# Stick-breaking attention: transposes two pieces behind the scores, contractions in quarters, and the causal mask on GpSimd

## The chip, the cores and the metric

The kernel runs on one core of a Trainium2 chip. Its engines are TensorE (PE for matmuls, PEld for its weight loads), VectorE (DVE), ScalarE (ACT), GpSimd (POOL) and SyncE (SP, which issues the DMAs). The metric is the device time of one execution in microseconds.

## What is computed

One decoder layer in float32 over 1024 tokens of width 1024: three token mixers beside each other (stick-breaking attention, mLSTM, cross-attention into a memory), merged by gates, and then a gated MLP. The change lies in the stick-breaking attention of 8 heads of width 64:

```python
z = einsum('bhtd,bhsd->bhts', q_block, k[:t1]) * scale
strict = arange(t1)[None, :] < (t0 + q_pos)[:, None]
log_fail = where(strict, log_sigmoid(-z), 0.0)
log_after = cumsum(log_fail, axis=3, reverse=True) - log_fail
w = where(strict, exp(log_sigmoid(z) + log_after), 0.0)
out = einsum('bhts,bhsd->bhtd', w, v[:t1])
```

A query sees earlier keys alone, strictly. For a masked key the factor sigmoid(-z) has to be 1 and the weight 0.

## The kernel before

The sequence is held in reverse, so the running product over later keys becomes a scan from left to right. Heads are worked in pairs (`p` = 0 to 3). A pair's scores are cut into 12 pieces, `PIECES`: a block of 128 queries (`rb`) by up to 512 keys (`o` is the first key block, counted from the diagonal; `w` is the width in keys). With `o == 0` a piece holds the diagonal block in its first 128 columns; that is so in 8 of 12 pieces, 32 of 48 in all.

One piece passes through these steps:

- `sb_weights`: scores of both heads on TensorE into the PSUM tile `z` (one buffer of two banks), each as two matmuls with split operands (L410, L413). On the diagonal a matmul of the identity with `mask` (0 or -1e30) stands between them (L412). ScalarE makes `f` = sigmoid(-z/8) (L415) and `g` = sigmoid(z/8) (L416), each in a buffer of the ring `U` (5 buffers). The first column of `f` is 1, by a memset on GpSimd (L418), or the carry of the piece before (L420). VectorE scans `f` to running products, one scan per head (L422), and multiplies `g` by them (L424).
- `sb_turn`: TensorE transposes `g` by blocks of 128 into the PSUM tile `tr` (one buffer, L434), ScalarE copies it to `y` (L436).
- `sb_apply`: TensorE contracts `y` with V (`sbv`) into the bank `pv` (L448); a finished bank is copied by ScalarE and stored (`store_y`, L395, L396).

Between these steps TensorE gets other work by generators, `chunks`: the projections of the next pair's Q and K (`proj_chunks`; evicted by `eq` and `ek` on ScalarE and VectorE), in the last pair the mLSTM's V (`nat_chunks`). A projection of one 512-wide half is 24 matmuls of three products (`mm3`, L149 to L151). A generator pauses after `k == 3` and at its end, so a chunk is half a contraction, 12 matmuls.

The loop over pieces (L604 to L625) sets the order in which instructions are written: scores, then a chunk in two of three pieces, then `apply_two` when two pieces are transposed, then the transposes of the piece before. A scheduler places the instructions engine by engine, near that order; weight loads have higher priority. Each engine works its queue in order. Behind the attention `gx_part` prepares the operands of the gate products, with four chunks drawn after each part.

Of the kernel before, what the change touches and what calls it, by code (L numbers as in the profile page):

```python
# [11 lines left out]
F32R = mybir.dt.float32r  # L12
AF = mybir.ActivationFunctionType
ALU = mybir.AluOpType
# [4 lines left out]
P = 128  # L19
# [10 lines left out]
NCH = S // P  # L30
# [12 lines left out]
def tile_hybrid_layer(ctx: ExitStack, tc: tile.TileContext, xT, memT, vecs, w_t, w_n, w_kv, w_if,  # L43
# [4 lines left out]
    nc = tc.nc  # L48
# [56 lines left out]
    def ts(t):  # L105
# [5 lines left out]
    ident_r = const.tile([P, P], F32R, tag="ident", name="ident")  # L111
    nc.vector.tensor_copy(ident_r, raw_id)
    ident = ident_r.bitcast(F32)

    raw_mask = T([P, P], "hf")
    nc.gpsimd.memset(raw_mask, 0.0)
    nc.gpsimd.affine_select(out=raw_mask, in_=raw_mask, pattern=[[1, P]], compare_op=ALU.is_gt, fill=-1e30,
                            base=0, channel_multiplier=-1)
    mask_r = const.tile([P, P], F32R, tag="mask", name="mask")
    nc.vector.tensor_copy(mask_r, raw_mask)  # L120
    ones = const.tile([P, P], F32, tag="ones", name="ones")
    nc.vector.memset(ones, 1.0)
    ones_r = const.tile([P, 2], F32R, tag="ones_r", name="ones_r")
# [211 lines left out]
    def proj_chunks(src, consume, halves=(1, 0)):  # L335

        with tc.high_priority(offset=SOON):
            wh, wl = wsplit(src)
        for h in halves:
            p = bank("pj")  # L340
            for k in range(KT):
                mm3(p, wh[:, ts(k)], wl[:, ts(k)], hh[k][:, hs(h)], hl[k][:, hs(h)], k == 0, k == KT - 1)
                if k == 3:
                    yield
            consume(h, p)
            yield

    def nat_chunks(which, consume, order=range(NCH - 1, -1, -1), ws=()):
        with tc.high_priority(offset=SOON):
            ws = list(ws) + [wsplit(w_n[which, b], None if b < 2 or ws else "pg") for b in range(len(ws), 4)]  # L350
        for t in order:
            p = bank("pj")
            for k in range(KT):
                wh, wl = ws[k // 2]
                mm3(p, hh[k][:, ts(t)], hl[k][:, ts(t)], wh[:, hs(k % 2)], wl[:, hs(k % 2)],
                    k == 0, k == KT - 1)
                if k == 3:
                    yield
            consume(t, p)
            yield  # L360
# [43 lines left out]
    def sb_weights(p, st, rb, o):  # L404
        qs, ks, kz = st
        w = min(4, NCH - rb - o) * P
        c = slice((rb + o) * P, (rb + o) * P + w)
        z = two("z")
        for a in range(2):
            nc.tensor.matmul(z[:, a, :w], qs[a][:, ts(rb)], ks[a][:, c], start=True, stop=False)  # L410
            if o == 0:
                nc.tensor.matmul(z[:, a, :P], ident_r, mask_r, start=False, stop=False, skip_group_check=True)  # L412
            nc.tensor.matmul(z[:, a, :w], qs[a][:, ts(rb)], kz[a][:, c], start=False, stop=True)  # L413
        f, g = T([P, 2, HALF + 1], "U"), T([P, 2, HALF], "U")
        nc.scalar.activation(f[:, :, 1:w + 1], z[:, :, :w], AF.Sigmoid, scale=-0.125)  # L415
        nc.scalar.activation(g[:, :, :w], z[:, :, :w], AF.Sigmoid, scale=0.125)  # L416
        if o == 0:
            nc.gpsimd.memset(f[:, :, 0:1], 1.0)  # L418
        else:
            nc.vector.tensor_copy(f[:, :, 0:1], carry[0])  # L420
        for a in range(2):
            nc.vector.tensor_tensor_scan(f[:, a, 1:w + 1], f[:, a, 1:w + 1], f[:, a, 1:w + 1],  # L422
                                         1.0 if o == 0 else f[:, a, 0:1], op0=ALU.mult, op1=ALU.bypass)
        nc.vector.tensor_mul(g[:, :, :w], g[:, :, :w], f[:, :, 0:w])  # L424
        carry[0] = f[:, :, w:w + 1]
        return g
# [45 lines left out]
    st, chunks = sb_qk(0)  # L472
# [116 lines left out]
        nc.sync.dma_start(v_d[t], v)  # L589


    weights, turned = [], []

    def turn_next():
        if weights:
            p, rb, o, g = weights.pop(0)
            turned.append((p, rb, o, sb_turn(rb, o, g)))

    def apply_two():
        if len(turned) == 2:  # L600
            for _ in range(2):
                sb_apply(*turned.pop(0))

    for p in range(4):  # L604
        now = st
        if p < 3:
            st, chunks = sb_qk(p + 1)
            chunks = chunks()
        else:
            chunks = nat_chunks(1, ev_v, [0, 1, 2, 3, 7, 6, 5, 4])  # L610
        for n, (rb, o) in enumerate(PIECES):
            g = sb_weights(p, now, rb, o)
            if n % 3 < 2:
                next(chunks, None)
            if (p, n) == (0, 2):
                next(rows_step)
            apply_two()
            turn_next()
            weights.append((p, rb, o, g))
        if p < 3:  # L620
            for _ in chunks:
                pass
    apply_two()
    turn_next()
    apply_two()  # L625

    spare.clear()
# [301 lines left out]

    for j in range(2):  # L930
        gx_part(j)
        for _ in range(4):
            next(chunks)
    go(3)
    LONG[:], SHORT[:] = ["pj"], ["pv"]
# [476 lines left out]
```

## Time and profile before

| what | value |
|---|---|
| runs, median (lowest to highest) | 1672.52 us (1671.65 to 1674.3) |
| profiled execution: time / span | 1671.65 us / 1669.6 us |
| TensorE matmuls busy | 1644.9 us (99%) |
| VectorE busy | 1209.9 us (72%) |
| ScalarE busy | 826.2 us (49%) |
| GpSimd busy | 53.4 us (3%) |
| scores of the attention, first to last start | 114.4 to 321.1 us |

Busy is the time in which at least one instruction of the engine runs. A matmul's duration covers its way through the array, while the next starts earlier: of matmuls in a row the distance of their starts is what each takes of TensorE's time. In rows of a timeline the columns are start, duration, engine, line, operation, output and inputs, shape, count, and in brackets the engine's idle time before it and what ended that.

### The profile page before, as it was taken

Reading aid. Unit: us, or ns where it says so; the run is one execution under the profiler, and the core shown is the slowest. Engines: PE = TensorE matmul, PEld = TensorE weight load, DVE = VectorE, ACT = ScalarE, POOL = GpSimd, SP = SyncE. Lnnn points to the kernel's source line nnn. Section 1 sums busy time; section 2 is a strip of 40 time slices with the busy share of each in tenths; the row PEclk is TensorE's granted clock in tenths of the full one; section 3 lists DMA queues with packets and bytes.
Section 4 is the critical chain, followed back from the end, with each engine's and each line's share of the span. In section 5 each row is a group of like instructions: output and inputs, shape, how many; then the busy total and the mean of one; then the engine's idle time right before and its main releaser. Section 6 shows DMA issues by size and latency. Waiting matters only on the chain.

```text
span 1669.6 us, 21196 instructions
## 1 busy us (share of the span) xinstructions
PE 1644.9 (99%) x7975; PEld 1338.8 (80%) x7975; DVE 1209.9 (72%) x1710; ACT 826.2 (49%) x1249; POOL 53.4 (3%) x95
## 2 busy tenths in 40 slices
PE   8999999999999999999999999999999999999999
PEld 4777777788877888888788888688888888788887
DVE  5648778777765666666567658997778877789864
ACT  4547667645555445656412334555555544543431
POOL 1000000010000001100000000000000000000000
PEclk9999999999999999999999999999999999999999
DMA  8421011234324665433855354222222221487141
GB/s 297 148 65 28 31 39 51 95 116 138 108 106 156 183 183 168 145 120 108 280 185 171 127 183 139 95 100 97 75 77 76 89 88 51 167 324 240 34 143 69
DMA packets 96249, 212.69 MB, mean 127 GB/s; under 512 B 12416, under 2 KB 36224, under 8 KB 96148
## 3 DMA queue, kind: packets, MB, share of 16 engines
q1 hardware_dynamic: 96148, 211.35, 37.3%
q8 instruction: 63, 1.03, 0.3%
q14 instruction: 38, 0.31, 0.1%
HBM read 156.71 MB, written 54.61 MB: 127 GB/s over the span
## 4 chain that ended last, share of the span: by engine, by line
PE 89%; DVE 4%; ACT 3%; DMA 2%; issue 1%; SPq 0%; POOLq 0%; ACTq 0%; DVEq 0%
PE ps_pj L149 14%; PE ps_pj L150 14%; PE ps_pj L151 14%; PE ps_pv L150 6%; PE ps_pv L151 6%; PE ps_pv L149 6%; PE ps_tr L149 4%; PE ps_tr L151 4%; PE ps_tr L150 4%; PE ps_z L149 3%; PE ps_z L150 3%; PE ps_z L151 3%; PE ps_tr L434 2%; PE ps_pv L448 1%; PE ps_z L226 1%; PE ps_z L413 1%
## 5 line engine op out<-in xcount | busy, mean ns | idle before, releaser
L150 PE MATMUL ps_pj<-h,whi 128*128 128x512 f32 x620 | 242.3, 391 | 0.0
L136 ACT ACTIVATE whi<-raw 128x512 fp32r<-128x512 f32 (+1 forms) x112 | 93.7, 836 | 180.3 <-PE ps_pj L150 84.8
L149 PE MATMUL ps_pj<-h,whi 128*128 128x512 f32 x412 | 163.0, 396 | 0.7 <-DVE U L1054 0.7
L149 PE MATMUL ps_pj<-pg,whi 128*128 128x512 f32 x396 | 154.7, 391 | 0.2 <-DVE pg L1052 0.2
L151 PE MATMUL ps_pj<-pg,wlo 128*128 128x512 f32 x380 | 148.0, 390 | 0.0
L150 PEld LDWEIGHTS ps_pj<-h,whi 128*128 128x128 f32 x620 | 116.5, 188 | 23.6 <-DVE U L287 0.2
L151 PE MATMUL ps_pj<-h,wlo 128*128 128x512 f32 x332 | 129.7, 391 | 0.0
L811 DVE SCALAR_TENSOR_TENSOR y<-U,vec,y 128x1023 f32<-128x1023 f32 x88 | 112.5, 1280 | 8.4 <-ACT y L809 8.4
L422 DVE TENSOR_TENSOR_SCAN U<-U 128x512 f32<-128x512 f32 (+3 forms) x96 | 88.6, 965 | 30.7 <-ACT U L415 29.8
L149 PEld LDWEIGHTS ps_pj<-h,whi 128*128 128x128 f32 x412 | 77.4, 188 | 17.2 <-DVE U L1054 1.1
L137 DVE TENSOR_TENSOR wlo<-raw,whi 128x1024 fp32r<-128x1024 f32 x54 | 66.0, 1223 | 30.8 <-ACT whi L136 30.6
L149 PEld LDWEIGHTS ps_pj<-pg,whi 128*128 128x128 f32 x396 | 74.4, 188 | 16.1 <-issue 0.5
L151 PEld LDWEIGHTS ps_pj<-pg,wlo 128*128 128x128 f32 x380 | 71.4, 188 | 14.9 <-issue 0.2
L136 ACT ACTIVATE whi<-pg 128x512 fp32r<-128x512 f32 (+1 forms) x59 | 43.4, 738 | 74.0 <-issue 21.2
L150 PE MATMUL ps_pj<-pg,whi 128*128 128x512 f32 x188 | 73.4, 390 | 0.0
L151 PEld LDWEIGHTS ps_pj<-h,wlo 128*128 128x128 f32 x332 | 62.4, 188 | 12.9
L150 PE MATMUL ps_pv<-h,whi 128*128 128x512 f32 x164 | 64.0, 390 | 0.0
L809 ACT ACTIVATE y<-U,vec 128x1024 f32<-128x1024 f32 x44 | 54.6, 1241 | 15.9 <-DVE U L713 14.4
L151 PE MATMUL ps_pj<-h,whi 128*128 128x512 f32 x156 | 60.8, 390 | 0.0
L137 DVE TENSOR_TENSOR wlo<-raw,wlo 128x512 fp32r<-128x512 f32 x58 | 39.9, 688 | 23.0 <-ACT wlo L136 22.9
L151 PE MATMUL ps_tr<-pg,wlo 128*128 128x512 f32 x144 | 56.2, 390 | 0.3 <-DVE wlo L137 0.3
L137 DVE TENSOR_TENSOR whi<-raw,whi 128x512 fp32r<-128x512 f32 x58 | 39.9, 688 | 21.8 <-ACT whi L136 21.8
(438 smaller groups left out, 4308.4 us busy)
## 6 DMA issues: line engine op xcount, KB each, us to landing
raw<-in_w_t_dram SPq DMA_DIRECT2D x29, 512.0 KB
gate_d<-U SPq DMA_DIRECT2D x24, 512.0 KB
U<-gate_d SPq DMA_DIRECT2D x24, 512.0 KB
pg<-in_w_up_dram SPq DMA_DIRECT2D x22, 512.0 KB
act_d<-y SPq DMA_DIRECT2D x22, 512.0 KB
pg<-in_w_t_dram SPq DMA_DIRECT2D x21, 512.0 KB
raw<-in_w_dn_dram SPq DMA_DIRECT2D x18, 512.0 KB
raw<-in_w_o_dram SPq DMA_DIRECT2D x16, 512.0 KB
```

Source lines behind the costliest of these rows:

```text
L136: nc.scalar.activation(hi, src, AF.Copy)
L137: (eng or nc.vector).tensor_sub(lo, src, hi.bitcast(F32))
L149: nc.tensor.matmul(out, lh, rh, start=start, stop=False, skip_group_check=more)
L150: nc.tensor.matmul(out, lh, rl, start=False, stop=False, skip_group_check=more)
L151: nc.tensor.matmul(out, ll, rh, start=False, stop=stop, skip_group_check=more)
L226: nc.tensor.matmul(pm[m], mg[k // 4][:, c], w[:, hs(kk)], start=(k == 0), stop=(k == KT - 1))
L413: nc.tensor.matmul(z[:, a, :w], qs[a][:, ts(rb)], kz[a][:, c], start=False, stop=True)
L422: nc.vector.tensor_tensor_scan(f[:, a, 1:w + 1], f[:, a, 1:w + 1], f[:, a, 1:w + 1], 1.0 if o == 0 else f[:, a, 0:1], op0=ALU.mult, op1=AL ...
L434: nc.tensor.transpose(pt[:, a, ts(j)], g[:, a, ts(j)], ident)
L448: nc.tensor.matmul(pv[64 * a:64 * a + 64, ts(rb % 4)], sbv[s // 2][:, s % 2, (2 * p + a) * 64:(2 * p + a + 1) * 64], wt[:, a, ts(j)], star ...
L809: nc.scalar.activation(out, u, AF.Identity, bias=bias, scale=taps[0])
L811: nc.vector.scalar_tensor_tensor(out[:, :S - s], u[:, s:], taps[s], out[:, :S - s], op0=ALU.mult, op1=ALU.add)
```

## The change

It has three parts.

1. The matmul with the mask goes, and with it the mask's constant. Instead GpSimd runs two selects (affine_select) behind the sigmoids of each diagonal piece: one puts 1 into the masked elements of `f`, the other 0 into those of `g`, in the first 128 columns of both heads.
2. The transposes are drawn two pieces behind the scores (they were one), ahead of the chunk instead of behind it. `apply_two` comes first.
3. The generators pause after `k` = 1, 3 and 5 as well as at the end: a chunk is a quarter, 6 matmuls. One quarter is drawn in the pieces 0, 1, 2, 3, 4, 6, 8 and 10 of a pair, two in the others, so none goes without. After the last pair four quarters stand between the last transposes and products, and each `gx_part` is followed by six quarters.

```diff
-    nc.gpsimd.memset(raw_mask, 0.0)
-    nc.gpsimd.affine_select(out=raw_mask, ...)
-    mask_r = const.tile([P, P], F32R, tag="mask", name="mask")
-    nc.vector.tensor_copy(mask_r, raw_mask)
...
@@ proj_chunks
-                if k == 3:
+                if k in (1, 3, 5):
                     yield
@@ nat_chunks(which, consume, order, ws, pauses=(3,))
-                if k == 3:
+                if k in pauses:
                     yield
@@ sb_weights
-            if o == 0:
-                nc.tensor.matmul(z[:, a, :P], ident_r, mask_r, start=False, stop=False, skip_group_check=True)
...
         if o == 0:
             nc.gpsimd.memset(f[:, :, 0:1], 1.0)
+            for t, fill in ((f[:, :, 1:P + 1], 1.0), (g[:, :, :P], 0.0)):
+                nc.gpsimd.affine_select(out=t, in_=t, pattern=[[0, 2], [1, P]], compare_op=ALU.is_gt, fill=fill,
+                                        base=0, channel_multiplier=-1)
@@ the loop over pieces
-            chunks = nat_chunks(1, ev_v, [0, 1, 2, 3, 7, 6, 5, 4])
+            chunks = nat_chunks(1, ev_v, [0, 1, 2, 3, 7, 6, 5, 4], pauses=(1, 3, 5))
         for n, (rb, o) in enumerate(PIECES):
             g = sb_weights(p, now, rb, o)
-            if n % 3 < 2:
+            if len(turned) == 2:
+                apply_two()
+            if len(weights) == 2:
+                turn_next()
+            weights.append((p, rb, o, g))
+            for _ in range(1 if n % 2 == 0 or n in (1, 3) else 2):
                 next(chunks, None)
...
-            apply_two()
-            turn_next()
-            weights.append((p, rb, o, g))
...
     apply_two()
     turn_next()
+    next(chunks)
+    next(chunks)
+    turn_next()
+    next(chunks)
+    next(chunks)
     apply_two()
...
     for j in range(2):
         gx_part(j)
-        for _ in range(4):
+        for _ in range(6):
             next(chunks)
```

First place: TensorE in the second head pair, around the transposes of piece (4,0), the first that is 512 keys wide (its weights `g` are `U_1486` before). The scores of piece (3,4) are the 128-wide ones (L410, L413), `ps_pj` is a projection. Before:

```order
L151 MATMUL ps_pj_1493<-h_108,wlo_1374 128x512
L434 MATMUL ps_tr_1553<-ident,U_1486 128x128 x8
L410 MATMUL ps_z_1564<-pg_835,pg_833 128x128
L413 MATMUL ps_z_1564<-pg_837,pg_833 128x128
L410 MATMUL ps_z_1564<-pg_836,pg_834 128x128
L413 MATMUL ps_z_1564<-pg_838,pg_834 128x128
L448 MATMUL ps_pv_1506<-y_1520,pg_548 64x128 x2
L448 MATMUL ps_pv_1506<-y_1520,pg_436 64x128 x4
L149 MATMUL ps_pj_1626<-h_101,whi_1622 128x512
L448 MATMUL ps_pv_1506<-y_1562,pg_548 64x128 x4
L448 MATMUL ps_pv_1506<-y_1562,pg_436 64x128 x4
```

The same place of TensorE in the changed kernel, whose lines are numbered otherwise: L403 and L404 are the scores, L429 the transposes, L142 to L144 the projection, and `U_1482` is the `g` of piece (4,0).

```order
L144 MATMUL ps_pj_1543<-h_95,wlo_1385 128x512
L403 MATMUL ps_z_1550<-pg_828,pg_826 128x128
L404 MATMUL ps_z_1550<-pg_830,pg_826 128x128
L403 MATMUL ps_z_1550<-pg_829,pg_827 128x128
L404 MATMUL ps_z_1550<-pg_831,pg_827 128x128
L429 MATMUL ps_tr_1563<-ident,U_1482 128x128 x8
L142 MATMUL ps_pj_1543<-h_96,whi_1384 128x512
L143 MATMUL ps_pj_1543<-h_104,whi_1384 128x512
L144 MATMUL ps_pj_1543<-h_96,wlo_1385 128x512
```

The transposes moved from ahead of the next piece's scores to behind them, and what follows them is a quarter of a projection, no longer products with V that read the copy of these very transposes (`y_1562`).

Second place: TensorE at the scores of the diagonal piece (3,0) of that pair. Before:

```order
L434 MATMUL ps_tr_1513<-ident,U_1464 128x128 x6
L410 MATMUL ps_z_1522<-pg_835,pg_833 128x512
L412 MATMUL ps_z_1522<-mask,ident 128x128
L413 MATMUL ps_z_1522<-pg_837,pg_833 128x512
L410 MATMUL ps_z_1522<-pg_836,pg_834 128x512
L412 MATMUL ps_z_1522<-mask,ident 128x128
L413 MATMUL ps_z_1522<-pg_838,pg_834 128x512
```

And in the changed kernel (L443 are products with V):

```order
L443 MATMUL ps_pv_1527<-y_1468,pg_429 64x128
L403 MATMUL ps_z_1510<-pg_828,pg_826 128x512
L404 MATMUL ps_z_1510<-pg_830,pg_826 128x512
L403 MATMUL ps_z_1510<-pg_829,pg_827 128x512
L404 MATMUL ps_z_1510<-pg_831,pg_827 128x512
L443 MATMUL ps_pv_1527<-y_1468,pg_429 64x128
L443 MATMUL ps_pv_1527<-y_1498,pg_429 64x128 x4
L429 MATMUL ps_tr_1534<-ident,U_1435 128x128 x6
```

The two mask matmuls are gone, and the transposes of piece (5,0) stand behind these scores.

Third place: GpSimd's queue at the beginning of the second pair; `U` are the buffers of `f` and `g`, `pg` those of the next pair's K. Before:

```order
L369 MEMSET pg_1352 64x1024
L370 MEMSET pg_1353 64x1024
L418 MEMSET U_1363 128x2
L418 MEMSET U_1408 128x2
L418 MEMSET U_1463 128x2
L418 MEMSET U_1485 128x2
```

In the changed kernel:

```order
L363 MEMSET pg_1337 64x1024
L410 MEMSET U_1345 128x2
L410 MEMSET U_1400 128x2
L412 AFFINE_SELECT U_1345<-U_1345 128x2x128
L412 AFFINE_SELECT U_1346<-U_1346 128x2x128
L410 MEMSET U_1434 128x2
L412 AFFINE_SELECT U_1400<-U_1400 128x2x128
L412 AFFINE_SELECT U_1401<-U_1401 128x2x128
L410 MEMSET U_1481 128x2
```

Each diagonal piece has two selects, and here the next piece's memset stands ahead of them.

More of the change, by code (lines that the diff above doesn't have):

```diff
@@ L113, in tile_hybrid_layer @@
     ident = ident_r.bitcast(F32)
-    raw_mask = T([P, P], "hf")
-    nc.gpsimd.memset(raw_mask, 0.0)
-    nc.gpsimd.affine_select(out=raw_mask, in_=raw_mask, pattern=[[1, P]], compare_op=ALU.is_gt, fill=-1e30,
-                            base=0, channel_multiplier=-1)
-    mask_r = const.tile([P, P], F32R, tag="mask", name="mask")
-    nc.vector.tensor_copy(mask_r, raw_mask)
     ones = const.tile([P, P], F32, tag="ones", name="ones")
@@ L346, in proj_chunks, with nat_chunks @@
             yield
-    def nat_chunks(which, consume, order=range(NCH - 1, -1, -1), ws=()):
+    def nat_chunks(which, consume, order=range(NCH - 1, -1, -1), ws=(), pauses=(3,)):
         with tc.high_priority(offset=SOON):
@@ L594, in turn_next @@
     def turn_next():
-        if weights:
-            p, rb, o, g = weights.pop(0)
-            turned.append((p, rb, o, sb_turn(rb, o, g)))
+        p, rb, o, g = weights.pop(0)
+        turned.append((p, rb, o, sb_turn(rb, o, g)))
     def apply_two():
-        if len(turned) == 2:
-            for _ in range(2):
-                sb_apply(*turned.pop(0))
+        for _ in range(2):
+            sb_apply(*turned.pop(0))
     for p in range(4):
```

## The prediction

> **What bounds the kernel now.** I read the page first (busy shares, then the chain), then the table by stages over the attention, then the waits of TensorE, then the timeline around the scores.
>
> ```profile
> span 1669.6 us, 21196 instructions
> PE 1644.9 (99%) x7975; PEld 1338.8 (80%) x7975; DVE 1209.9 (72%) x1710; ACT 826.2 (49%) x1249; POOL 53.4 (3%) x95
> PE 89%; DVE 4%; ACT 3%; DMA 2%; issue 1%; SPq 0%; POOLq 0%; ACTq 0%; DVEq 0%
> ```
>
> TensorE is busy all the way and holds 89% of the chain that ended last. So an instruction taken off TensorE shortens the run, and so does each of its waits that goes; work given to another engine costs nothing until TensorE waits for it. The change touches only the attention, whose first scores start at 114.6 us and whose last product ends near 331. One row for each of the four head pairs follows (elapsed; busy of PE, PEld, DVE, ACT, POOL; clock; DMA share; GB/s):
>
> ```profile
> 114.60:167.40 52.80, 50.00 (x343) 40.40 (x341) 46.84 (x84) 39.56 (x55) 2.48 (x8) 1.00 0.12 36
> 167.40:220.40 53.00, 51.84 (x377) 42.08 (x376) 41.61 (x51) 37.31 (x52) 2.67 (x10) 1.00 0.09 30
> 220.40:273.40 53.00, 51.80 (x378) 42.08 (x376) 41.55 (x51) 37.22 (x53) 0.82 (x8) 1.00 0.09 31
> 273.40:331.00 57.60, 55.57 (x422) 45.23 (x421) 42.43 (x48) 35.22 (x48) 0.71 (x7) 1.00 0.27 90
> ```
>
> TensorE stands idle 2.80, 1.16, 1.20 and 2.03 us there, 7.2 together. VectorE is second: 41.6 of 53.0 in a middle pair, 46.84 of 52.80 in the first, where the gate rows of the mLSTM are worked out beside it. GpSimd has almost nothing. What TensorE waits for between 114 and 332 (total, times, longest):
>
> ```profile
> PE ps_tr L434 <- DVE U L424: 3.7, 5, 1.6
> PE ps_pv L448 <- ACT y L436: 1.6, 3, 0.5
> PE ps_z L410 <- ACT U L416: 1.0, 1, 1.0
> ```
>
> The transposes wait for the product of weights on VectorE (L424), the contraction with V for ScalarE's copy of the transposes, and once the scores for the sigmoids to empty `z`.
>
> **Part 1: the mask matmuls go (64 of them).** Rows of TensorE: one head's scores with the mask and what follows them, then one head's without.
>
> ```profile
> 131.66 0.40 PE L410 MATMUL ps_z<-pg,pg 128*128 128x512 f32 x1
> 131.89 0.23 PE L412 MATMUL ps_z<-mask,ident 128*128 128x128 f32 x1
> 131.95 0.44 PE L413 MATMUL ps_z<-pg,pg 128*128 128x512 f32 x1
> 132.24 0.39 PE L149 MATMUL ps_pj<-h,whi 128*128 128x512 f32 x1
> ...
> 162.24 0.40 PE L413 MATMUL ps_z<-pg,pg 128*128 128x512 f32 x1
> 162.47 0.39 PE L410 MATMUL ps_z<-pg,pg 128*128 128x512 f32 x1
> 162.70 0.39 PE L413 MATMUL ps_z<-pg,pg 128*128 128x512 f32 x1
> ```
>
> Durations overlap, so the price is the distance of starts. With the mask one head takes 131.66 to 132.24, 0.58 us; without it two matmuls take 162.24 to 162.70, 0.46. The mask costs 0.12: 0.06 of its own (131.89 to 131.95), and 0.06 by which the matmul behind it is stretched (0.29 against 0.23). Times 64 that is 7.7 us; the lower end, its own 0.06 alone, is 3.8. I take 7.7, since both rows show the stretch. The Trainium skill, page "TensorE: Matmul & The Clock Gate", section "Back-to-back issue gap", gives 81 ns for a 128-column matmul in a stream with weight loads; by it the 64 would be worth an estimated 5.2 us. The rows here measure 0.12 and decide. The memset, select and cast that made the mask run in the first microseconds, before TensorE starts; they count as nothing.
>
> **Part 2: the transposes move back by a piece, the contractions are cut into quarters.** No matmul is added or lost by this. What goes are waits.
>
> ```profile
> 170.40 1.06 PE L434 MATMUL ps_tr<-ident,U 128*128 128x128 f32 x8 [0.44 <-DVE U L424]
> ...
> 191.28 1.09 PE L448 MATMUL ps_pv<-y,pg 128*64 128x128 f32 x16 [0.54 <-ACT y L436]
> ...
> 326.94 1.06 PE L434 MATMUL ps_tr<-ident,U 128*128 128x128 f32 x8 [1.56 <-DVE U L424]
> ```
>
> The first two recur in each later pair, 53 us apart; the third is the tail, where no contraction was left between. After the change all three have a contraction quarter or more ahead of them, and the transposes of 170.40 stand behind another step. The idle of the last three pairs is 1.16 + 1.20 + 2.03 = 4.4 us as the page counts it. A matmul is written 0.39 long while its successor starts 0.23 later, so each wait hides another 0.16: with some twelve waits 1.9 more. I take 6.3 us for these. The first pair's 2.8 I leave standing: VectorE is nearly full there, and the order lets the early transposes stand close behind their scores as before.
>
> Two things move with this. On SyncE the first pair's store of products now stands ahead of the third weight load, so the load waits for the store's data:
>
> ```profile
> 139.13 0.35 SPq L142 DMA_DIRECT2D raw<-in_w_t_dram  x1
> 139.96 0.34 SPq L396 DMA_DIRECT2D y_d<-me  x1
> ```
>
> They are 0.8 us apart, and the weights are used only in the next pair, from 167 us on: nothing, unless the store came 20 us late. And of the last projection twelve quarters remain behind the attention, where eight halves did: 5.5 us less cover (24 matmuls at 0.23) for the loads and splits of the gate operands there. Behind them stand other contractions:
>
> ```profile
> 340.00:380.00 40.00, 40.00 (x179) 33.12 (x178) 27.54 (x39) 19.41 (x32) 8.71 (x11) 1.00 0.30 98
> ```
>
> TensorE has no idle there, the first step of three units runs before those operands are read: nothing.
>
> One place gets tighter. Piece (4,0), the first that is 512 wide, shows the chain of today:
>
> ```profile
> 181.16 1.03 ACT L415 ACTIVATE U<-ps_z 128x1024 f32<-128x1024 f32 x1 [1.01 <-PE ps_z L413]
> 182.08 1.02 ACT L416 ACTIVATE U<-ps_z 128x1024 f32<-128x1024 f32 x1
> ...
> 182.22 2.34 DVE L422 TENSOR_TENSOR_SCAN U<-U 128x512 f32<-128x512 f32 x2 [0.33 <-ACT U L415]
> 184.69 1.23 DVE L424 TENSOR_TENSOR U<-U,U 128x1024 f32<-128x1024 f32 x1
> 186.58 2.34 DVE L422 TENSOR_TENSOR_SCAN U<-U 128x512 f32<-128x512 f32 x2 [0.66 <-ACT U L415]
> ```
>
> From the first sigmoid to the end of the product are 181.16 to 185.92, 4.8 us, and 5.3 with a select in it. On TensorE, by the new order, there lie between these scores and their transposes 12 contraction matmuls (2.7), 4 and 6 transposes, 6 products with V, and two blocks of scores: about 6 us. That is closer than now (188.07 against scores that ended near 181), so 0 to 0.5 us of wait per pair may come here.
>
> **Part 3: two selects on GpSimd per diagonal piece (32 pieces, 64 selects).** None of 128x2x128 is in the trace. The nearest rows are one of 128 elements and eight of 512 (min, median, max):
>
> ```profile
> L117 POOL TENSOR_SCALAR_AFFINE_SELECT hf<-hf 128x128 f32<-128x128 f32 x1 | 0.3, 292 | 0.0
> ...
> L856 POOL TENSOR_SCALAR_AFFINE_SELECT me<-me x8: 634/640/1689, 377.9 to 648.6; 128x512 f32<-128x512 f32 x8
> ```
>
> Between 292 and 640 ns, 256 elements come to 0.41; the ends are those two. GpSimd does 6.6 us of it in a pair of 49, so it is no bound. The memset at the head of each piece's buffer stands in the same queue, ahead of selects:
>
> ```profile
> POOL U L418 <- PE ps_tr L434: 107.6, 17, 26.1
> ```
>
> It waits for transposes to free the buffer, and now selects are queued behind it. By the order this holds for the first three pieces of a pair alone, and the transposes in question are those two pieces back, done within the step; these pieces are narrow. I count nothing.
>
> What can hurt is the 1.69 among the eight selects. GpSimd's row, VectorE's around it, and a second meeting:
>
> ```profile
> 452.26 1.69 POOL L856 TENSOR_SCALAR_AFFINE_SELECT me<-me 128x512 f32<-128x512 f32 x1 [72.66 <-ACT y L809]
> ...
> 452.17 1.28 DVE L811 SCALAR_TENSOR_TENSOR y<-U,cw,y 128x1023 f32<-128x1023 f32 x1 [0.44 <-ACT y L809]
> 453.37 0.68 DVE L713 TENSOR_TENSOR U<-U,ps_pv 128x512 f32<-128x512 f32 x1
> 453.96 1.28 DVE L811 SCALAR_TENSOR_TENSOR y<-U,cw,y 128x1022 f32<-128x1022 f32 x1
> ...
> 631.41 0.64 POOL L856 TENSOR_SCALAR_AFFINE_SELECT me<-me 128x512 f32<-128x512 f32 x1 [1.31 <-DMA me<-me_d]
> ...
> 630.74 0.69 DVE L137 TENSOR_TENSOR whi<-hf,whi 128x512 fp32r<-128x512 f32 x1
> 631.47 1.12 DVE L694 TENSOR_TENSOR hf<-pg 128x512 f32<-128x512 f32 x1
> ```
>
> At 452 the select ends only at 453.95, half a microsecond after the VectorE operation that had begun before it (452.17 to 453.45); the operation with an operand in PSUM at 453.37 is not held, and the next with two operands in SBUF starts at 453.96. At 631 the select came first, and a 0.69 us operation took 1.12. So a select and a VectorE operation with two SBUF inputs exclude each other. The Trainium skill, page "SBUF — State Buffer", section "SBUF: two separate sides", says so: VectorE and GpSimd share a port pair as an exclusive lock, which two-input VectorE operations hold against a GpSimd operation that reads SBUF. These rows agree; whether a scan counts as two-input none shows.
>
> The price for VectorE: at 631 0.43 of a 0.64 us select; for one of 0.41 that leaves 0.2 (low end, and nothing where VectorE idles anyway). High end: the 0.51 between 453.45 and 453.96, taken whole. I take 0.25, nearest the low row because that one is scaled to the size. Sixteen selects in a pair add 4 us: 41.6 becomes 45.6, and with some 1.6 us between scans and their products (2.47 from start to start at 182.22, against 2.34 busy) 47.2. TensorE needs 53.0 - 1.9 (mask) - 1.7 (waits) = 49.4 in a middle pair. VectorE stays under it by 2 us, too little to hide every collision: so I add 0.5 us of new waits to each of the four pairs, the tight place above among them: 2.0.
>
> **Sum.** Against the profiled run's own 1671.65 us (span 1669.6): -7.7 -6.3 +2.0 = -12.0, so 1659.7. The median of the three runs is 0.9 above that run, so I say 1660.
>
> **Rivals.** *VectorE becomes the bound.* At 0.51 a select, middle pairs need 41.6 + 1.6 + 8.2 = 51.4 on VectorE and gain 1.6 each; the first (46.8 + 8.2) gains nothing, the last, which is short of VectorE work before its tail, 4. Gain about 7: 1665. For it: scans fill VectorE and may hold the lock too. Against: VectorE now idles 11.4 us in a middle pair. By the lock rule of the Trainium skill's page "SBUF — State Buffer" this is the case to expect, if a scan counts as two-input.
>
> *Every wait goes.* The mask's 7.7 and all waits, 7.2 + sixteen times 0.16 = 9.8: 17.5 us, 1655; should the page understate the waits more than that, 1653. For it: selects that land in VectorE's idle time cost nothing. Against: the first pair.
>
> *Slower: the second select stalls the product.* It must find a gap in the scans of its own piece (2.34 us), and the product L424 stands behind it in VectorE's queue. If the two selects cost a diagonal piece 1.2 us on VectorE, a middle pair is at 41.6 + 1.6 + 9.6 = 52.8 and nothing is gained; from there on it is slower. At 1.6 us, 56 in the middle pairs (+3 each) and 61 in the first, of which one piece's slack hides 4 (+4), less 2 in the last: +8, 1680. For it: the 1.69 us select. Against: that one lost its 1.05 while VectorE worked, not idled.
>
> *No change*, the same mechanism near 1.2 us: the mask's 7.7 comes back as waits for L424.
>
> **How the numbers follow.** Forecast 0.42, VectorE bound 0.22, every wait gone 0.20: these are faster, 0.84. No change (within 0.2%, about what a measurement of this kernel can tell) 0.09, slower 0.07. The range 1653 to 1668 holds the first three, down to the last one's lower figure and up to 3 us beyond VectorE's case for a dearer select.
>
> **What would show it.** Right: no L412, scores that follow each other at 0.23; the four rows by pair each shorter by 1.9 or more; idle before transposes near nothing in the later pairs and no wait in the tail; selects near 0.4 us when alone. VectorE's case: its busy time above 50 of a pair, scans or products recorded longer than 1.2 us, and TensorE's waits on L424 grown past 3.7. Wrong altogether: selects of 1 us and more with VectorE idle behind them, or a TensorE wait for `z` or `U` in every piece.

## The result and the profile after

The changed kernel took 1661.57 us (median of six, 1658.55 to 1663.46) where the kernel before took 1673.05 beside it (six, 1671.65 to 1674.53): a ratio of 0.993, 95% interval 0.9919 to 0.9941. Repeated at the end of the study it took 1659.76 against 1674.08, 0.9917 (0.9904 to 0.9931). The forecast was 1660, within 1653 to 1668. The profiled execution of the changed kernel took 1658.55 us, 13.1 less than that of before, and its span 12.8 less.

The head of the page after (span, busy times, the chain that ended last):

```profile
span 1656.8 us, 21182 instructions
PE 1635.1 (99%) x7911; PEld 1333.6 (80%) x7911; DVE 1212.9 (73%) x1709; ACT 823.5 (50%) x1249; POOL 93.3 (6%) x157
PE 87%; DVE 3%; ACT 1%; DMA 1%; issue 0%; POOLq 0%; POOL 0%; ACTq 0%
```

64 matmuls are gone from TensorE, GpSimd works 40 us more, and VectorE 3 us more in its sum. The table by pairs, cut at the first scores of each pair as the one of before (the last row ends with the last product of the attention):

```profile
114.90:163.70 48.80, 45.50 (x286) 36.40 (x285) 45.99 (x82) 36.21 (x51) 12.96 (x25) 0.97 0.09 28
163.70:212.60 48.90, 48.90 (x362) 40.78 (x361) 43.30 (x51) 36.89 (x53) 12.30 (x26) 1.00 0.09 33
212.60:261.50 48.90, 48.90 (x362) 40.77 (x361) 42.92 (x51) 37.87 (x54) 10.88 (x24) 1.00 0.10 34
261.50:322.40 60.90, 60.12 (x462) 49.93 (x460) 48.26 (x54) 39.49 (x55) 11.01 (x23) 1.00 0.28 96
```

The two middle pairs went from 53.0 to 48.9 us, and TensorE has no idle in them: elapsed and busy time are equal. The first pair kept 3.30 us of idle, and its mean clock is 0.97. The fourth row is longer than before because more lies in it: the transposes and products of two pieces that used to be done within the first pair are deferred from pair to pair (together about 2.5 us), and four quarters of the last projection stand before the last product (24 matmuls, 5.5 us). What TensorE waits for between 113 and 330 us, and the longest wait that the selects bring to another engine:

```profile
PE ps_tr L429 <- DVE U L419: 2.5, 3, 1.3
PE ps_z L403 <- ACT U L407: 0.8, 1, 0.8
PE ps_tr L429 <- ACT y L431: 0.8, 1, 0.8
...
DVE U L417 <- POOL U L412: 15.8, 17, 2.2
```

The first two lines are all of the first pair, the third stands at 267.39 in the fourth. The scans (L417) now wait for the selects where they waited for the sigmoids before (29.8 us then); TensorE does not feel it. The scores without the mask follow each other at 0.23:

```profile
195.02 0.39 PE L403 MATMUL ps_z<-pg,pg 128*128 128x512 f32 x1
195.25 0.40 PE L404 MATMUL ps_z<-pg,pg 128*128 128x512 f32 x1
195.49 0.39 PE L403 MATMUL ps_z<-pg,pg 128*128 128x512 f32 x1
195.72 0.40 PE L404 MATMUL ps_z<-pg,pg 128*128 128x512 f32 x1
```

### The profile page after: what moved, and what is told of

Read it like the earlier page. It is cut to its first block, busy times and chain, and to the rows that moved or that the text cites. A ratio compares the mean times of both kernels' runs of the same rounds, so it can differ in the third digit from the quotient of the medians.

```text
span 1656.8 us, 21182 instructions
## 1 busy us (share of the span) xinstructions
PE 1635.1 (99%) x7911; PEld 1333.6 (80%) x7911; DVE 1212.9 (73%) x1709; ACT 823.5 (50%) x1249; POOL 93.3 (6%) x157
## 4 chain that ended last, share of the span: by engine, by line
PE 87%; DVE 3%; ACT 1%; DMA 1%; issue 0%; POOLq 0%; POOL 0%; ACTq 0%
PE ps_pj L142 13%; PE ps_pj L143 13%; PE ps_pj L144 13%; PE ps_pv L143 6%; PE ps_pv L142 6%; PE ps_pv L144 6%; PE ps_tr L142 4%; PE ps_tr L144 4%; PE ps_tr L143 4%; PE ps_z L142 3%; PE ps_z L143 3%; PE ps_z L144 3%; PE ps_pv L443 2%; PE ps_tr L429 2%; PE ps_z L403 1%; PE ps_z L404 1%
## 5 line engine op out<-in xcount | busy, mean ns | idle before, releaser
L142 PE MATMUL ps_pj<-h,whi 128*128 128x512 f32 x412 | 165.0, 400 | 0.0
L142 PE MATMUL ps_pj<-pg,whi 128*128 128x512 f32 x396 | 154.8, 391 | 0.3 <-DVE pg L1053 0.2
L144 PE MATMUL ps_pj<-pg,wlo 128*128 128x512 f32 x380 | 147.9, 389 | 0.0
L144 PE MATMUL ps_pj<-h,wlo 128*128 128x512 f32 x332 | 130.3, 392 | 0.0
L417 DVE TENSOR_TENSOR_SCAN U<-U 128x512 f32<-128x512 f32 (+3 forms) x96 | 92.9, 1008 | 17.5 <-POOL U L412 15.8
L142 PEld LDWEIGHTS ps_pj<-h,whi 128*128 128x128 f32 x412 | 77.6, 188 | 15.5 <-issue 0.3
L130 DVE TENSOR_TENSOR wlo<-raw,whi 128x1024 fp32r<-128x1024 f32 x54 | 65.9, 1221 | 32.2 <-ACT whi L129 32.0
L142 PEld LDWEIGHTS ps_pj<-pg,whi 128*128 128x128 f32 x396 | 74.4, 188 | 16.6 <-DVE pg L1053 0.8
L144 PEld LDWEIGHTS ps_pj<-pg,wlo 128*128 128x128 f32 x380 | 71.4, 188 | 14.8 <-issue 0.2
L144 PEld LDWEIGHTS ps_pj<-h,wlo 128*128 128x128 f32 x332 | 62.6, 189 | 13.2
L144 PE MATMUL ps_pj<-h,whi 128*128 128x512 f32 x156 | 60.8, 390 | 0.0
L406 ACT ACTIVATE U<-ps_z 128x1024 f32<-128x1024 f32 (+3 forms) x48 | 39.0, 813 | 40.5 <-PE ps_z L404 32.7
L130 DVE TENSOR_TENSOR wlo<-raw,wlo 128x512 fp32r<-128x512 f32 x58 | 39.8, 686 | 22.3 <-ACT wlo L129 22.1
L144 PE MATMUL ps_tr<-pg,wlo 128*128 128x512 f32 x144 | 56.1, 389 | 0.0
```

The costliest lines, as they stand in the source:

```text
L130: (eng or nc.vector).tensor_sub(lo, src, hi.bitcast(F32))
L142: nc.tensor.matmul(out, lh, rh, start=start, stop=False, skip_group_check=more)
L144: nc.tensor.matmul(out, ll, rh, start=False, stop=stop, skip_group_check=more)
```

## The experiments

The clearest measure is the period of a pair, from its first scores to those of the next, read from each run's timeline. It repeats to about 0.1 us in the middle pairs. "Rest" is the span from the fourth pair's first scores to the end, as a difference from the kernel before; it varies by some microseconds between executions, so a small one says little. Where no interval stands, the kernel ran once.

| kernel | first | second | third | rest | ratio to before (95%) |
|---|---|---|---|---|---|
| before | 52.82 | 53.04 | 53.11 | 0 | 1 |
| changed | 48.77 | 48.90 | 48.90 | -0.7 | 0.993 (0.9919 to 0.9941) |
| changed, repeated | 48.57 | 48.93 | 48.95 | -0.3 | 0.9917 (0.9904 to 0.9931) |
| e1: before, mask matmuls out | 51.09 | 51.51 | 51.52 | +1.7 | 0.9966 (0.9954 to 0.9977) |
| e2: before, mask by selects | 52.68 | 52.02 | 51.97 | -0.6 | 0.9984 (0.9974 to 0.9993) |
| e3: new order, mask on TensorE | 52.09 | 50.69 | 50.69 | +3.5 | 0.9978 (0.9968 to 0.9987) |
| e4: changed, selects out | 47.63 | 48.87 | 48.87 | +0.9 | 0.9917 (0.9902 to 0.9931) |
| e5: changed, each select twice | 50.11 | 50.30 | 49.77 | +2.7 | 0.9956 (0.9942 to 0.9971) |
| e6: changed, gate rows drawn late | 49.08 | 48.87 | 48.93 | +4.9 | 0.9918 (0.9901 to 0.9935) |
| e7: changed, halves for quarters | 51.00 | 51.25 | 51.25 | +1.4 | 1666.51 us, once |
| e8: changed, transposes one behind | 57.43 | 57.16 | 57.13 | +5.6 | 1689.66 us, once |
| e9: changed, memsets for selects | 47.45 | 48.89 | 48.95 | -1.2 | 1656.98 us, once |
| e10: changed, gate rows after the attention | 47.73 | 49.06 | 49.02 | +9.1 | 0.996 (0.9946 to 0.9974) |
| e11: e10 and an early sigmoid table | 45.00 | 49.09 | 49.03 | +7.9 | 0.9938 (0.9926 to 0.9951) |

### The parts by themselves: e1 to e4

e1 takes the mask matmuls out of the kernel before and puts nothing in their place (no causal mask on the diagonal):

```diff
-            if o == 0:
-                nc.tensor.matmul(z[:, a, :P], ident_r, mask_r, start=False, stop=False, skip_group_check=True)
```

> The kernel before with the 64 mask matmuls left out and nothing in their place, so masked weights stay in the output; no other line changes. Theory (a mask matmul costs TensorE 0.12 us, its own slot and the stretch of the matmul behind it): 7.7 us less, 6.5 to 8.5, and a middle head pair of 51.1 us in place of 53.0. Rival (only the slot of 0.06 counts): 3.8 us less, a pair of 52.0.

e2 does the same and adds the selects: the whole first part of the change in the old order.

```diff
+            for t, fill in ((f[:, :, 1:P + 1], 1.0), (g[:, :, :P], 0.0)):
+                nc.gpsimd.affine_select(out=t, in_=t, pattern=[[0, 2], [1, P]], ...)
```

> The kernel before with the mask moved to GpSimd, but its old order: halves of contractions, transposes one piece behind. Theory (the two parts are nearly independent, and the select adds 0.5 us to the chain from scores to transposes, which the old order hides in all but two or three places of a pair): 4 to 6 us less than before. Rival (the mask can move only together with the later transposes, since the chain is already late in the old order): 0 to 2 us less, with the waits for the product of weights grown from 3.7 to 10 us or more.

e3 is the changed kernel with the mask back on TensorE and without selects: the order and the quarters alone.

```diff
+            if o == 0:
+                nc.tensor.matmul(z[:, a, :P], ident_r, mask_r, start=False, stop=False, skip_group_check=True)
...
-            for t, fill in ((f[:, :, 1:P + 1], 1.0), (g[:, :, :P], 0.0)):
-                nc.gpsimd.affine_select(...)
```

> The changed kernel with the mask matmul back on TensorE and no select. Theory: the waits go as they did, the mask stays: 13.1 - 7.7 = 5.4 us less than before, 4.5 to 6.5, a middle pair of 50.8 us with no idle. Rival (the later order was needed only for the select): 0 to 2 us less.

e4 is the changed kernel without the selects (no causal mask on the diagonal).

```diff
-            for t, fill in ((f[:, :, 1:P + 1], 1.0), (g[:, :, :P], 0.0)):
-                nc.gpsimd.affine_select(...)
```

> The changed kernel with the two selects of each diagonal piece left out, so masked weights stay in the output. Theory (TensorE is the bound of the three later pairs and the selects cost only in the first pair, where VectorE is nearly full): 1 to 2 us faster than the changed kernel, 14 to 15 us less than before, and the middle pair stays at 48.9 us. Rival (collisions of selects and scans still cost in every pair): 3 us or more faster than the changed kernel, the middle pair under 48.5.

The second pair of e1, e2, e3 and e4, in this order, each from its own table by pairs:

```profile
166.90:218.40 51.50, 50.12 (x361) 40.11 (x360) 41.65 (x51) 37.10 (x52) 2.65 (x10) 1.00 0.09 32
```

```profile
166.70:218.70 52.00, 50.14 (x361) 40.11 (x360) 43.00 (x51) 37.04 (x52) 15.13 (x26) 1.00 0.10 31
```

```profile
167.40:218.10 50.70, 50.70 (x378) 42.95 (x377) 41.86 (x51) 36.91 (x53) 2.66 (x10) 1.00 0.09 32
```

```profile
162.80:211.70 48.90, 48.90 (x362) 40.79 (x361) 42.42 (x51) 36.96 (x53) 2.73 (x10) 1.00 0.10 33
```

TensorE idles 1.38 and 1.86 us in the old order (e1, e2), and not at all in the new one (e3, e4). So the new order takes away the waits of a middle pair with or without the mask matmuls, and 16 mask matmuls cost 50.69 - 48.87 = 1.82 us there, 0.11 each. In the old order the same 16 were worth only 53.07 - 51.51 = 1.56: a quarter of a microsecond came back as waits.

The two parts are worth more together than apart. The order alone gives 2.38 a middle pair and the mask by selects alone 1.08, which makes 3.46; together they give 4.17. A quarter of a microsecond of the difference is the one just named; the larger part is what the selects cost. In the old order they lengthen the way from the sigmoids to the product, and the transposes wait for that product 7.3 us in all where it was 3.7 before and 3.1 in e1 (e2):

```profile
PE ps_tr L429 <- DVE U L419: 7.3, 8, 1.5
```

That is 0.5 us of a middle pair (e1 to e2). In the new order the transposes stand two pieces behind, and the selects cost 0.0 there (e4's 48.87 against 48.90).

In these middle pairs e3 and e4 met their theories; the whole times were forecast less well. By medians against the kernel before, e1 is 5.2 us faster (6.5 to 8.5 expected), e2 2.6 (between its theory and its rival), e3 3.2 (4.5 to 6.5) and e4 13.5 (14 to 15). And e2 and e3 together make 5.8, where the change made 11.5 and 14.3 in its two measurements: much of what the two parts gain only together lies in the first pair (-0.14 and -0.73 apart, -4.05 together), where e3 still has 4.7 us of idle and a slower clock for 3.4 us. That part was not taken to pieces.

### How much room is left: e5, e7, e8

e5 runs every select twice, to the same effect:

```diff
-            for t, fill in ((f[:, :, 1:P + 1], 1.0), (g[:, :, :P], 0.0)):
+            for t, fill in 2 * ((f[:, :, 1:P + 1], 1.0), (g[:, :, :P], 0.0)):
```

> The changed kernel with both selects of each diagonal piece run twice, which changes nothing of the result. Theory (selects and VectorE's two-input operations exclude each other, and in the changed kernel VectorE has about 3 to 5 us of a middle pair left): sixteen more selects at 0.25 to 0.5 us add 4 to 8 us to VectorE, so it becomes the bound, a middle pair takes 50 to 53 us in place of 48.9, and the kernel is 4 to 12 us slower than the changed one. Rival (the selects only fill idle time of both engines): the middle pair stays within 0.5 us of 48.9.

e7 keeps the new order, but lets the generators pause at half a contraction, as before:

```diff
-                if k in (1, 3, 5):
+                if k == 3:
...
-            for _ in range(1 if n % 2 == 0 or n in (1, 3) else 2):
+            if n % 3 < 2:
                 next(chunks, None)
```

> The changed kernel with the generators pausing at halves as before, one half drawn in two of three pieces, transposes still two pieces behind and the select on GpSimd. Theory (the later transposes take away the waits, and quarters only spread what is drawn): a middle pair of 49.5 to 50.5 us, since scores that follow a piece without a chunk wait for the sigmoids to empty their buffer. Rival (quarters matter as much as the later transposes): 51 us or more. Second rival: 48.9, no difference.

e8 keeps the quarters and draws the transposes one piece behind the scores:

```diff
-            if len(weights) == 2:
+            if weights:
                 turn_next()
```

> The changed kernel with the transposes one piece behind the scores, as before, but quarters and the select kept. Theory (the later transposes are what hides the longer chain): scores, then at once the transposes of the piece before, whose product is not ready: waits for VectorE's product in most pieces, a middle pair of 53 us or more. Rival (the quarters alone do it): 49 to 50.

For each of the three, its second pair and what TensorE waited for over the attention. e5:

```profile
165.50:215.80 50.30, 49.14 (x361) 40.85 (x360) 43.99 (x51) 37.01 (x53) 22.15 (x43) 1.00 0.09 32
...
PE ps_tr L429 <- DVE U L419: 5.8, 7, 1.3
```

e7:

```profile
164.80:216.10 51.30, 50.19 (x361) 40.73 (x361) 43.14 (x51) 36.86 (x53) 15.35 (x26) 1.00 0.09 32
...
PE ps_z L403 <- ACT U L407: 3.0, 6, 0.8
```

e8:

```profile
171.90:229.10 57.20, 51.15 (x361) 40.77 (x361) 43.19 (x51) 37.23 (x53) 13.21 (x26) 1.00 0.08 29
...
PE ps_tr L429 <- DVE U L419: 12.1, 17, 1.4
PE ps_tr L429 <- DVE U L415: 8.4, 12, 1.2
```

In e5 a middle pair slowed by 0.9 to 1.4 us. VectorE is not what fills it: it works 43.99 of 50.30. It is the way through a piece: two more selects lie between its sigmoids and its product, and the transposes wait for the product again. All of the second pair's idle is one such wait, at piece (4,0). GpSimd's queue has a share in it: there the selects of (4,0) start only at 181.06, though their sigmoid ends at 179.35, because the next piece's memset stands ahead of them and waits until a product has freed its buffer (rows of GpSimd, then of TensorE):

```profile
180.96 0.10 POOL L410 MEMSET U<- 128x2 f32 x1 [1.96 <-DVE U L419]
181.06 6.06 POOL L412 TENSOR_SCALAR_AFFINE_SELECT U<-U 128x256 f32<-128x256 f32 x8
...
186.16 1.06 PE L429 MATMUL ps_tr<-ident,U 128*128 128x128 f32 x8 [1.16 <-DVE U L419]
```

So the changed order has room for the two selects of a diagonal piece, but not for two more.

In e7 and e8 the same selects and the same matmuls stand in another order, and a middle pair takes 51.25 and 57.1. With halves, scores come up before the sigmoids have emptied `z`; with the transposes one piece behind, those wait for products (L419) and, as the profile names it, for copies of the carry (L415). e7 came out as its first rival said, not its theory. Both halves of the new order are needed: the quarters are worth 2.3 us of a middle pair, the second piece of distance (given quarters) 8.2. In e8 the transposes also stand ahead of the chunk, where the kernel before had them behind it, so the 8.2 is for distance and place together; quarters with the transposes one piece behind and after the chunk were not tried.

### Whether scans and selects exclude each other: e9

Alone, a select of 256 elements takes 0.407 us in the changed kernel, but 22 of the 64 took over 0.6, and one 2.7 (line, engine, count, ns min/median/max, first and last start):

```profile
L412 POOL TENSOR_SCALAR_AFFINE_SELECT U<-U x64: 400/407/2706, 120.1 to 305.4; 128x256 f32<-128x256 f32 x64
```

GpSimd's and VectorE's rows around two of those:

```profile
127.40 0.90 POOL L412 TENSOR_SCALAR_AFFINE_SELECT U<-U 128x256 f32<-128x256 f32 x1 [0.29 <-ACT U L407]
131.24 3.14 POOL L412 TENSOR_SCALAR_AFFINE_SELECT U<-U 128x256 f32<-128x256 f32 x2 [0.51 <-ACT U L407]
...
127.14 1.97 DVE L417 TENSOR_TENSOR_SCAN U<-U 128x384 f32<-128x384 f32 x2 [0.50 <-POOL U L412]
131.41 2.32 DVE L417 TENSOR_TENSOR_SCAN U<-U 128x512 f32<-128x512 f32 x2
133.77 0.69 DVE L370 TENSOR_TENSOR pg<-ps_pj,pg 64x512 fp32r<-64x512 f32 x1
```

The first of the two selects at 131.24 ends near 133.95, only after both scans (131.41 to 133.73), which pass back to back at their usual length. It is the only one of the 64 that took over 1.5 us: the select at 127.40 got its turn between two scans and ended at 128.30, and the second of those took 1.09 us where the first took 0.96. The second select of 131.24 runs beside an operation with an operand in PSUM and is not held. If a select is held because it reads SBUF, then a memset of the same elements, which only writes, must not be. e9 replaces the selects by memsets in the same places (the diagonal blocks of `f` and `g` are set whole, so no causal mask):

```diff
-                nc.gpsimd.affine_select(out=t, in_=t, pattern=[[0, 2], [1, P]], ...)
+                nc.gpsimd.memset(t, fill)
```

> The changed kernel with each select replaced by a memset of the same columns, so the whole first block of a diagonal piece is masked and the output is not the reference's: GpSimd writes as much as before but reads nothing. Theory (VectorE's two-input operations, scans among them, hold off a GpSimd operation that reads): every memset takes one short time, none is stretched to 0.9 us or more, and no scan of 512 is recorded above 1.25 us, where the selects were stretched 22 times in 64. Rival (any GpSimd access to the same buffers collides with scans): memsets stretched as the selects were.

```profile
L412 POOL MEMSET U<- x64: 311/313/322, 120.3 to 304.2; 128x256 f32 x64
```

None of the 64 is stretched, though they stand among the same scans. So reading is what collides, and scans hold off a select that reads. The kernel gives a scan `f` for both of its inputs (L417), so it is an operation with two inputs in SBUF, which the prediction had left open. The other direction is weak. Of the 48 scans of 512 elements, 23 took more than 1.25 us with the selects (up to 1.44) and 8 with the memsets (up to 1.29), as in the kernel before and in e4: the few long ones are not the selects' doing, the other 15 are. In VectorE's busy time of a middle pair the 16 selects show as 43.30 against 42.42 (e4), 0.05 us each, and 32 as 43.99, 0.05 each again.

The Trainium skill, page "SBUF — State Buffer", section "SBUF: two separate sides", gives the rule of the shared port for VectorE operations with two SBUF inputs against a GpSimd operation that reads SBUF. These runs agree, for scans whose two inputs are one tensor in SBUF.

### The first pair: e6, e10, e11

The 3.3 us of idle that stay in the first pair lie before 137 us, beside the gate rows of the mLSTM, which VectorE works out there. Part of what follows them is a slower clock (rows of TensorE):

```profile
120.39 0.39 PE L403 MATMUL ps_z<-pg,pg 128*128 128x256 f32 x1 [0.79 <-ACT U L407]
...
122.67 0.55 PE L429 MATMUL ps_tr<-ident,U 128*128 128x128 f32 x2 [1.07 <-DVE U L419]
...
123.45 0.63 PE L142 MATMUL ps_pj<-h,whi 128*128 128x512 f32 x1
123.88 0.63 PE L143 MATMUL ps_pj<-h,whi 128*128 128x512 f32 x1
```

Behind the two waits, matmuls start 0.43 apart instead of 0.23 for 3.4 us; the granted clock reads 0.5 there. That is some 1.6 us. The repeat of the changed kernel has the drop again (at 123.3), and e6 (at 122.8); e3, without a select, has one at 135.3 and e10 one at 121.9. The other runs have none in this pair. The two waits do not decide it alone, for e8 has the same two and keeps its full clock behind them:

```profile
120.00 0.39 PE L403 MATMUL ps_z<-pg,pg 128*128 128x256 f32 x1 [0.79 <-ACT U L407]
...
122.29 0.44 PE L429 MATMUL ps_tr<-ident,U 128*128 128x128 f32 x2 [1.07 <-DVE U L419]
```

What decides it stays open. One such drop takes 0.001 off the mean granted clock of an execution, and that mean reads 0.999 in two of the changed kernel's six executions and 1.000 in four, and 0.999 in two of the four of e4, without selects. So the drop comes and goes with one and the same kernel, and it can't be put down to the selects. With it goes the difference between the profiled first pairs: 48.77 and 48.57 (the changed kernel) against 47.63 and 47.45 (e4, e9). TensorE idles no less in e4's first pair (3.77 us against 3.30), but its matmuls take 1.7 us less:

```profile
115.20:162.80 47.60, 43.83 (x286) 35.39 (x285) 45.40 (x82) 35.98 (x51) 2.52 (x8) 1.00 0.09 28
```

e6 draws the first step of the gate rows in the fourth pair:

```diff
-            if (p, n) == (0, 2):
+            if (p, n) == (3, 2):
                 next(rows_step)
```

> The changed kernel with one edit: the first step of the gate rows, VectorE's extra work in the first pair, is drawn in the fourth pair. Theory (VectorE is what TensorE waits for in the first pair): the first pair, 48.8 us, gets 1.5 to 3 us shorter, the fourth no longer, the kernel 1.5 to 3 us faster than the changed one, 13 to 15 us less than before. Rival (the first pair's waits come from the chain of its first pieces, with no work ahead of them, not from VectorE's load): under 0.7 us.

```profile
L514 DVE TENSOR_TENSOR mw<-mw x14: 213/270/408, 116.0 to 135.9; 32x127 f32<-32x127 f32 x2, 32x126 f32<-32x126 f32 x2, 32x124 f32<-32x124 f32 x2, 32x120 f32<-32x120 f32 x2
```

The rows still ran from 116 to 136 us: the scheduler put them forward. So e6 is another run of nearly the same kernel and tells nothing of its theory. e10 makes the gate rows depend on the last weights of the attention (a copy from the last `g` is written where their inputs land) and draws them behind both `gx_part`:

```diff
+        for t in (gi, gf):
+            nc.vector.tensor_copy(t[:, 0:1], held[0])
...
-            if (p, n) == (0, 2):
-                next(rows_step)
...
+    held[0] = g_last
+    next(rows_step)
     go(3)
```

> The changed kernel with the gate rows' first step held back behind the attention, by a small copy that reads the last piece's weights (drawing it later in the code had moved nothing, since the scheduler put it forward again). Theory (VectorE's load of the first pair, 46 us of 48.8, makes TensorE wait there): the first pair at 45.5 to 47.5 us, the kernel 1 to 3 us faster than the changed one. Rival (the first waits come from ScalarE's evictions and from loading its table ahead of the first sigmoids): the first pair within 0.7 us of 48.8.

e11 also loads the sigmoid's table at the start, by a small activation:

```diff
-    nc.scalar.activation(warm, nhalf[:, :1], AF.Square)
+    nc.scalar.activation(warm, nhalf[:, :1], AF.Sigmoid)
```

> As the run before, and the warm-up activation at the kernel's start is a sigmoid, so no table is loaded ahead of the first scores. Theory: both causes add, the first pair at 44 to 46.5 us, the kernel 2 to 5 us faster than the changed one, 14 to 17 us less than before. Rival (no waits of the first pair hang on the table): the same as the run before, within 0.4 us in the first pair.

The first pair became 47.73 and then 45.00 us. In e10 TensorE no longer waits there for a product of VectorE, but its wait for the first sigmoids grew from 0.79 to 2.42 us; the pair came out between the theory and the rival. In the changed kernel and in e10 ScalarE loads the sigmoid's table right ahead of the first sigmoid (below, the changed kernel's row), and in e11 that load is gone and the wait is 1.13 us. The other half of e11's gain is that it lacks e10's drop of the clock:

```profile
118.38 1.28 ACT L406 ACT_TABLE_LOAD   x1
```

But both kernels lost more behind the attention than they won: 7.2 and 3.9 us slower than the changed kernel beside them, where 1 to 3 and 2 to 5 faster had been expected. In e10 ScalarE reaches the gate rows' exponential while its input is still on the way, and everything queued behind it waits; TensorE's longest wait there is for an eviction in that queue (rows of ScalarE and of TensorE's waits, then 20 us of e10's table):

```profile
369.29 1.28 ACT L565 ACT_TABLE_LOAD   x1 [8.74 <-DMA sm<-mp_d]
...
PE ps_pj L142 <- ACT U L704: 3.3, 1, 3.3
...
365.00:385.00 20.00, 16.75 (x67) 13.36 (x66) 5.95 (x9) 8.29 (x16) 2.27 (x4) 0.91 0.25 80
```

In the changed kernel TensorE is busy 19.29 us of that stretch at full clock. So the gate rows are well placed in the first pair after all: moving them won one microsecond there (48.77 to 47.73) and cost some 9 us here. The early table alone, with the gate rows where they are, was not tried; their logarithm loads a table at 112.46, ahead of the first sigmoid, so the early one would presumably be displaced again.

Last, the changed kernel again, to see how its ratio repeats:

> The changed kernel once more, beside the version with late gate rows on the same chip: 11 to 13 us less than before by the median, pairs of 48.8, 48.9 and 48.9 us.

It came to 0.9917 (0.9904 to 0.9931), the same as e4 and within 0.0001 of e6: 14.3 us less than before, somewhat more than expected, with the pairs as expected. Only e9, without the causal mask, was lower; no kernel with the whole computation was clearly faster than the changed one.

## Why the prediction was right

The forecast case came about, and its sum of -12.0 stands against -12.8 of the span. By pairs, with the 2.5 us that are deferred from the first to the last taken back: the first -1.5, the middle ones -4.14 and -4.21, the rest -3.2, and the first scores start 0.3 later. The sum is closer than its terms: the mask and the waits were put some 0.7 us too high (14.0 against about 13.3), the new waits some 1.5 too high (2.0 against the 0.5 that are left), so part of the fit is luck. By medians the two measurements gave 11.5 and 14.3 less, so a difference of 0.8 says nothing. Step by step:

- **The mask, 64 times 0.12 = 7.7 us.** Measured: 0.11 (e3 against the changed kernel, 1.8 a pair), 7.2. It was right to price the stretched successor too; the row's own 0.06 would have given half.
- **Waits, 6.3 us.** Right in sum, misplaced: the middle pairs lost 53.07 - 1.82 - 48.90 = 2.35 each, where 1.2 of idle and about 0.6 hidden in overlapping matmuls had been counted; the hidden part was 1.1 (TensorE's busy time of 51.84 before against 50.70 in e3, with the mask matmuls in both). The last pair brought about 1.4 beyond its mask instead of over 2 (no better known than the rest of the span, which varies), for one wait of 0.78 stayed there, for ScalarE's copy at 267.39. The tail has no wait left, as forecast.
- **New waits, +2.0 us, half a microsecond in each pair.** This is the mis-sized term. The middle pairs got none: idle 0.00, and taking the selects away changes 48.90 to 48.87. The first pair idles no longer than without the selects (3.30 us against e4's 3.77); the 1.1 us by which it is longer (48.77 against 47.63) go with the drop of the clock, which can't be put down to the selects.
- **0.25 us on VectorE for each select.** Too dear: 0.05 (e4, e5). The prediction let VectorE pay half the price of each meeting; the runs show that GpSimd pays most of it. It is busy 12.30 us in the second pair against 2.73 in e4, 0.60 for each select of 0.41, and GpSimd has time.
- **The tight place, piece (4,0).** The scan now waits for the select there (1.41 us of VectorE's idle at 177.98), and the transposes do not wait. Its slack is real but small: e5's two extra selects used it up.
- **The memset ahead of the selects, counted as nothing.** Right for TensorE, but not as described: in the changed kernel 23 of its 27 waits are for VectorE to free the buffer (products, L419, and carry copies, L415) and only 4 for transposes. It costs nothing until the chain is longer, as in e5.
- **The store ahead of the third weight load on SyncE, counted as nothing.** The load went from 139.13 to 146.53, and TensorE waited for nothing in the pair that uses it. The store, issued at 141.57, is not what held it: by the profile the load waited 4.5 us longer, for VectorE's split of the weights before (`wlo`, L130, 145.29 to 146.51) to free its buffer.

```profile
141.57 0.34 SPq L389 DMA_DIRECT2D y_d<-me  x1
146.53 21.14 SPq L135 DMA_DIRECT2D raw<-in_w_t_dram  x2
```

The rivals: *VectorE the bound* did not come, with 43.3 busy of 48.9. Its premise, that scans hold selects off, is true (e9); its price was wrong by a factor of ten. *Every wait goes* is right for the middle pairs and the tail and fails in the first pair, where 3.30 us of idle stayed. *The second select stalls the product* did not come: in e2 VectorE's scans wait for the first select (24.0 us in all) and no product waits for the second; in e5 products wait for it 0.5 us in all. What is seen of it is a chain that the selects lengthen, at 0.5 us a middle pair in the old order (e2) and 0.9 to 1.4 in e5; in the changed kernel the two pieces of distance cover it. *No change* would have needed it dearer still.

## What to carry to other kernels

Price an instruction in a pipelined stream by the distance of starts with it and without it, its successor included. Before a step is moved to an idle engine, look how much slack the chain has in which it lands, not only how busy that engine is: the same two selects cost 0.5 us a pair where the consumer stood close and nothing where it stood a piece further back, so two edits can be worth more together than the sum of each. A long contraction can be cut as finely as the waits that it is to cover; here halves against quarters made 2.3 us a pair.

## What was not expected of the hardware

A select that meets scans is held, up to behind two in a row (2.7 us for 0.41, once; the others took at most 1.42), while the scans lose almost nothing; the half-microsecond between VectorE operations that the trace of before showed at 453 was no measure for that. And TensorE's clock fell to half for 3.4 us behind two waits of 0.8 and 1.1 us that lay 2.3 us apart, which cost some 1.6 us more than the waits show; behind the same two waits in e8 it did not fall. In e10 the same fall came behind a wait of 2.42 us (at 121.9) and one of 3.3 us (at 374.4).
